# Token mixing: softmax division moved from GpSimd to ScalarE, three other wide element operations from GpSimd to VectorE

## The chip, the cores and the metric

One NeuronCore of a Trainium2 chip runs the kernel. Its engines work side by side, each through its own queue in order: TensorE (PE in the profile; its weight loads are PEld), VectorE (DVE), ScalarE (ACT), GpSimd (POOL) and SyncE (SP), which issues nearly all DMAs. The metric is device time in microseconds of one execution; the median of the runs counts.

## The reference

One layer of a streaming encoder, for a prompt of 2048 tokens and 8 sampled sequences of 16 tokens, model width 1024, all in float32:

```python
# x @ w_in gives q, k, v, output gate of 4 mLSTM heads (128 wide), 8 gate columns,
# and q (8 heads x 64), k, v (2 heads x 64) of a sliding-window attention
hm = mlstm_chunkwise(qm, km, vm, logi, logf, C0, n0, m0, chunk)   # matrix memory, exact per token
hm = sigmoid(om) * head_norm(hm)
qa, ka = rope(qa), rope(ka)
s = q k^T / 8, masked to the own chunk of 64 and two before
mx = max(max(s), sink);  p = exp(s - mx);  p = p / (sum(p) + exp(sink - mx));  ha = p v
h = layer_norm(alpha * x + concat(hm, ha) @ w_out)
u = h @ w_up;  c = causal conv of width 3;  f = (silu(c_gate) * c_value) @ w_down
y = layer_norm(alpha * h + f)
```

The outputs are y, the new memories and the last rows of keys, values and of u.

## The kernel before

A float32 product is made of three products of rounded numbers (a high and a low part of each side): the high part of a tile is a copy on ScalarE (L217, L562, L892), the low part a subtraction on VectorE (L218, L563, L893). The large products also save multiplications by a two by two scheme of sums of blocks, so their results are collected in three PSUM banks A, B and C that are evicted and added in a fixed order.

Tokens come in 17 tiles of 128 (16 of the prompt, one of the samples). Three stages follow each other on TensorE:

- the input projection (up to about 690 us) in four blocks of tiles. Its products are L700; `i_after` evicts the banks between them, on ScalarE (`i_out`'s L756 and L759, the copies L767, L775 and L795) and on VectorE (L771, L773). A product may begin only when the bank it writes has been evicted. Projected rows go to DRAM through SP (L749 for the attention queries, the output gate and v).
- the output projection and the first layer norm (about 690 to 960 us) in five blocks (L222 to L224, eviction L1607). `x_pair` (L880) loads pairs of mixed features and splits them.
- the feed-forward part, up-projection and down-projection (from 960 us).

The token mixing of each tile, mLSTM (`m_tile`, `m_norm`) and attention (`swa`), is woven between the matmuls of the first two stages: `Chains.weave` advances generators by an estimate of TensorE's time. This fixes the order of all TensorE instructions by hand; the order on the other engines is made by a planner that lays each instruction where its own estimate of times puts it. All small results of TensorE in the mixing share five PSUM banks in turn (`bank`), so a transposition may have to wait until a bank of an earlier step has been read.

Places that the change and the prediction touch:

- `swa`: `scores` makes masked scores and their maxima on VectorE (L1292 to L1297), `exps` the exponentials with their sums on ScalarE (L1301, L1303), `divided` adds the sink's part to the sums and takes the reciprocal on VectorE (L1306, L1307) and multiplies four heads by it on GpSimd (L1308). This is done twice a tile, for half of the heads each. TensorE then transposes the quotients (L1330) into banks called ppt.
- `m_tile`: VectorE makes sd and kw (L1122, L1191), GpSimd multiplies the queries by the weights of the state, qk by wi (L1192), TensorE uses both (L1199, L1200, L1207), VectorE reads the banks (statistics L1140, L1141, state L1210, values L1146). ScalarE's L1143 reads the same banks.
- `rope`: three products on VectorE (L864 to L866), and the sum on the engine that is handed in as `adder` (L867): VectorE for the keys of the prompt, GpSimd for the queries.
- `x_pair`: the low part (L893) on GpSimd for every second pair of the first four blocks, else on VectorE.

Of the kernel before, what the change touches and what calls it, by code (L numbers as in the profile page):

```python
# [8 lines left out]
F32 = mybir.dt.float32  # L9
F32R = mybir.dt.float32r  # L10
AF = mybir.ActivationFunctionType
# [3 lines left out]
P = 128  # L15
# [24 lines left out]
IBLOCKS = [[0, 1, 2, 3, 16], [4, 5, 6, 7], [8, 9, 10, 11], [12, 13, 14, 15]]  # L40
# [164 lines left out]
class Prog:  # L205
# [524 lines left out]
    def i_keys(self, b, ti, ps):  # L730
        nc = self.nc
        t = IBLOCKS[b][ti]
        kv = self.zev()[:, :2 * P]
        nc.scalar.copy(kv, ps[:, 8:264])
        nc.scalar.copy(self.gates[b][:, ti, :], ps[:, :8])
        self.rope(kv[:, :P], t, 1, nc.vector)
        nc.sync.dma_start(self.zkv[t], kv)

    def i_store(self, b, g, i, j, ev):
# [11 lines left out]
    def i_out(self, b, g, i, j, src):  # L751

        nc = self.nc
        ev = src if i else self.zev()
        if g == 3:
            nc.scalar.activation(ev, src, AF.Tanh, scale=0.5)  # L756
            nc.vector.tensor_scalar_add(ev, ev, 1.0)
        elif not i:
            nc.scalar.copy(ev, src)  # L759
        if g == 2:  # L760
            self.rope(ev, IBLOCKS[b][2 * j], 2, nc.gpsimd)
        self.i_store(b, g, i, j, ev)

    def i_after(self, b, g, s):
# [32 lines left out]
    def i_batch(self, g):  # L797

        nc = self.nc
        ps = self.sb.pop(g)  # L800
        t = NPT
        ev = self.zev()
        if g == 2:
            nc.scalar.copy(ev, ps)
            self.rope(ev, t, 1, nc.gpsimd)
            nc.sync.dma_start(self.zqa[t], ev)
            return
        if g < 2:
            nc.scalar.copy(ev[:, :HT], ps[:, :HT])
            nc.scalar.activation(ev[:, HT:], ps[:, HT:], AF.Copy, scale=KSCALE)  # L810
            self.trans = g, ev
            return
        if g == 3:
            nc.scalar.activation(ev, ps, AF.Tanh, scale=0.5)
            nc.vector.tensor_scalar_add(ev, ev, 1.0)
        else:
            nc.scalar.copy(ev, ps)
        nc.sync.dma_start((self.zog, self.zv)[g - 3][t], ev)
# [32 lines left out]
        nc.sync.dma_start(self.zt[0, k], x)  # L851
        nc.sync.dma_start(self.zt[1, k], y)

    def rope(self, A, t, nt, adder):

        V = self.nc.vector
        n = A.shape[-1]
        B = self.mp.tile([P, 512], F32, name="rb", tag="rb", bufs=1)[:, :n]
        r, i0 = self.angles[t]
        cos, ms, sin = [r[:, i0:i0 + nt, i:i + 1, :] for i in range(3)]  # L860
        w = A.rearrange("p (t x d) -> p t x d", t=nt, d=32)
        h = lambda z, s: z.rearrange("p (t h s d) -> p t h s d", t=nt, s=2, d=32)[:, :, :, s]
        over = lambda z: z.to_broadcast([P, nt, n // (64 * nt), 32])
        V.tensor_mul(h(B, 0), h(A, 1), over(ms))  # L864
        V.tensor_mul(h(B, 1), h(A, 0), over(sin))
        V.tensor_mul(w, w, cos.to_broadcast([P, nt, n // (32 * nt), 32]))  # L866
        adder.tensor_add(A, A, B)  # L867

    def rope_load(self, t, nt):

# [9 lines left out]
    def x_pair(self, b, p):  # L880

        nc, nb = self.nc, len(OBLOCKS)
        W = len(OBLOCKS[b]) * P
        if p == 0:
            for t in OBLOCKS[b]:
                self.chains.until(t)
        raw = self.xp.tile([P, 2, 512], F32, name="xraw", tag=f"xr{p + 1}", bufs=1)[:, :, :W]
        nc.sync.dma_start(raw, self.zmix[b][2 * p:2 * p + 2].rearrange("k p m -> p k m"))
        s = (7, 6, 5, 3, 4)[self.xn % 5]
        self.xn += 1  # L890
        h, l = [self.xp.tile([P, 2, 512], F32R, name=n, tag=f"{n}{s}", bufs=1)[:, :, :W] for n in ("oh", "ol")]
        nc.scalar.copy(h, raw)  # L892
        (nc.gpsimd if b < nb - 1 and p % 2 else nc.vector).tensor_sub(l, raw, h.bitcast(F32))  # L893
        self.xs.setdefault(b, []).extend((h[:, i], l[:, i]) for i in range(2))

    def group(self, b, tiles, u0, last):
# [278 lines left out]
    def m_tile(self, t, load, i, mp):  # L1175
        nc = self.nc
        V = nc.vector
        qk, v1, og = load
        pm = self.m_rep(i)
        col = self.m_cols(i, mp)  # L1180
        dt = self.m_masked(pm, self.mcau)
        yield 600, 2800
        emt = self.m_emt(col)
        wi = self.m_inter(pm, col)
        self.m_exps(dt, col)
        yield 0, 5000, 2
        ps = self.m_scores(qk)
        kt = self.m_ktok(qk)
        sd = self.m_weighted(ps, dt)
        kw = self.work("kw", [P, MH, P])  # L1190
        V.tensor_mul(kw, kt, dt[:, :, P - 1:P].to_broadcast([P, MH, P]))  # L1191
        nc.gpsimd.tensor_mul(qk[:, 0:4], qk[:, 0:4], wi)  # L1192
        yield 950, 4000, 4
        num = []
        for j in range(2):
            ps = self.bank([P, 2, 129], "pnum")
            for i in range(2):
                h = 2 * j + i
                nc.tensor.matmul(ps[:, i], sd[:, h], v1[:, h], start=True, stop=False)  # L1199
                nc.tensor.matmul(ps[:, i], qk[:, h], self.C[:, h], start=False, stop=True)  # L1200
            num.append(ps)
        Cn = self.work("C", [P, MH, 129], bufs=2)
        for j in range(2):
            ps = self.bank([P, 2, 129], "pcu")
            for i in range(2):
                h = 2 * j + i
                nc.tensor.matmul(ps[:, i], kw[:, h], v1[:, h], start=True, stop=True)  # L1207
            for i in range(2):
                h = 2 * j + i
                V.scalar_tensor_tensor(Cn[:, h], self.C[:, h], wi[:, h, P - 1:P], ps[:, i], op0=ALU.mult, op1=ALU.add)  # L1210
        self.C = Cn
        return num, emt, og
# [45 lines left out]
    def swa(self, t):  # L1258
        nc = self.nc
        V = nc.vector  # L1260
# [14 lines left out]
        N = nk * P  # L1275
        mix = self.work("mixa", [P, 4, P])

        def scores(j0):

            sink = [x.rearrange("p (k j) -> p k j", k=2)[:, :, j0:j0 + 2] for x in (self.sink, self.nsink)]  # L1280
            sc = self.work("sc", [P, 4, 2 * P], bufs=2)
            mx, es, sm = [self.work(n, [P, 4], bufs=2) for n in ("amx", "aes", "asm")]
            ps = [self.bank([P, 2, 2, P], "psc") for _ in range(2)]
            for j in range(2):
                for i, (q, k) in enumerate(((qh, self.kh), (qh, self.kl), (ql, self.kh))):
                    for kvh in range(2):
                        rs = slice(64 * kvh, 64 * kvh + 64)
                        nc.tensor.matmul(ps[kvh][:, j, :nk], q[rs, j0 + j], k[rs, sel], start=i == 0, stop=i == 2)  # L1288
            for kvh in range(2):
                for j in range(2):  # L1290
                    c = 2 * kvh + j
                    V.tensor_tensor_reduce(out=sc[:, c, :N], in0=ps[kvh][:, j, :nk].rearrange("p a b -> p (a b)"), in1=mask, scale=1.0, scalar=-3e38,  # L1292
                                           op0=ALU.add, op1=ALU.max, accum_out=mx[:, c:c + 1])

            w = lambda x: x.rearrange("p (k j) -> p k j", k=2)
            V.scalar_tensor_tensor(w(mx), w(mx), -0.125, sink[1], op0=ALU.mult, op1=ALU.min)
            V.tensor_add(w(es), sink[0], w(mx))  # L1297
            return sc, mx, es, sm

        def exps(sc, mx, es, sm):  # L1300
            nc.scalar.activation(es, es, AF.Exp)  # L1301
            for j in range(4):
                nc.scalar.activation(sc[:, j, :N], sc[:, j, :N], AF.Exp, bias=mx[:, j:j + 1], scale=0.125, accum_out=sm[:, j:j + 1])  # L1303

        def divided(sc, mx, es, sm):
            V.tensor_add(sm, sm, es)  # L1306
            V.reciprocal(sm, sm)  # L1307
            nc.gpsimd.tensor_mul(sc[:, :, :N], sc[:, :, :N], sm.rearrange("p (h o) -> p h o", o=1).to_broadcast([P, 4, N]))  # L1308

        z = [scores(0)]  # L1310
        yield 900, 3200, 2
        exps(*z[0])
        z.append(scores(2))
        yield 900, 3600
        divided(*z[0])
        exps(*z[1])
        if t + 1 < NPT and self.i_done > self.place(t + 1)[0]:
            self.a_load = self.swa_dma(t + 1)
        yield 0, 3000
        divided(*z[1])  # L1320
        scs = [x[0] for x in z]
        yield 0, 4200, 2 + 2 * (self.a_load is not None)
# [804 lines left out]
```

## Time and profile before

| | us |
|---|---|
| median of 3 runs | 2399.57 (2395.45 to 2402.28) |
| the profiled execution | 2395.7 |
| its span, first to last instruction | 2393.9 |

The profiled execution is 1.8 us longer than its span, and 3.9 us below the median. Of the span TensorE is busy 97%, VectorE 78%, ScalarE 52%, GpSimd 14%. A row of the groups reads: line, engine, operation, tile written and tiles read, shapes, count, then busy time in us and the mean duration in ns of one, then idle time of the engine just before, with who ended it. A row of waits reads: who waited, for whom, us in total, how often, the longest. A row of the stretches reads: the stretch, its length, then each engine's busy time with its count, the granted TensorE clock, the DMA share and GB/s. A row of the timeline reads: start, duration, engine, line, operation, and in brackets the idle time before it.

### The profile page before, as it was taken

How to read it: one execution, taken by the hardware profiler on the slowest of the kernel's cores; microseconds unless marked ns; L12 is line 12 of the kernel's file. 1: busy time of each engine (PE TensorE's matmuls, PEld its weight loads, DVE VectorE, ACT ScalarE, POOL GpSimd, SP SyncE). 2: the span in 40 equal slices, each digit the busy share in tenths (PEclk: the TensorE clock that was granted, in tenths of full speed). 3: DMA queues.
4: the chain of work that ended last, by engine and by line, in shares of the span. 5: the costliest groups of instructions: out<-in, count | busy, mean ns of one | idle time of the engine just before them, and what ended most of it. 6: DMA issues, size and time to landing. Idle time of an engine off the chain costs nothing.

```text
span 2393.9 us, 39845 instructions
## 1 busy us (share of the span) xinstructions
PE 2326.6 (97%) x14425; PEld 2128.9 (89%) x14425; DVE 1860.4 (78%) x3180; ACT 1233.6 (52%) x2295; POOL 347.1 (14%) x354
## 2 busy tenths in 40 slices
PE   8999999999999999999999999999999999999998
PEld 8999998988887777999999999999999978778776
DVE  8676587687789897987788777768766786895987
ACT  5453455655554444655556555455544544544553
POOL 0101103112222331300000000002100100310400
PEclk9999999999999999999999999999999999999999
DMA  8798888789877656687776889888988786756652
GB/s 287 261 315 291 280 294 311 261 263 328 288 247 241 204 197 240 252 308 281 283 271 240 312 315 316 306 270 269 318 284 262 227 284 203 233 174 223 226 172 106
DMA packets 296934, 624.98 MB, mean 261 GB/s; under 512 B 47005, under 2 KB 140193, under 8 KB 296737
## 3 DMA queue, kind: packets, MB, share of 16 engines
q1 hardware_dynamic: 294144, 612.99, 75.3%
q0 software_dynamic: 1728, 6.29, 0.7%
q10 hardware_dynamic: 864, 3.15, 0.3%
q8 instruction: 114, 1.87, 0.3%
q14 instruction: 84, 0.68, 0.1%
HBM read 451.78 MB, written 170.56 MB: 260 GB/s over the span
## 4 chain that ended last, share of the span: by engine, by line
PE 68%; DVE 10%; DMA 4%; issue 3%; ACT 2%; POOL 1%; SPq 0%; DVEq 0%; POOLq 0%; ACTq 0%
PE dps L1830 18%; PE fup L1830 17%; PE dps L700 6%; PE fht L2033 5%; PE dps L2033 5%; PE fup L2033 4%; PE dps L222 2%; PE dps L223 2%; PE dps L224 2%; DMA txy<-wdn 1%; DVE w L218 1%; DVE uw L218 1%; PE ppo L1336 1%; PE ppt L1330 1%; PE psc L1288 1%
## 5 line engine op out<-in xcount | busy, mean ns | idle before, releaser
L1830 PE MATMUL dps<-hh,uw 128*128 128x384 f32 (+1 forms) x1848 | 481.6, 329 | 7.0 <-ACT u L1855 1.9
L1830 PE MATMUL fup<-hh,uw 128*128 128x384 f32 (+1 forms) x1848 | 479.9, 328 | 2.0 <-ACT u L1855 1.8
L1830 PEld LDWEIGHTS dps<-hh,uw 128*128 128x128 f32 x1848 | 330.1, 188 | 10.8 <-ACT u L1855 3.0
L1878 DVE SCALAR_TENSOR_TENSOR cc<-u,cw,cc 128x768 f32<-128x768 f32 (+1 forms) x264 | 252.5, 977 | 106.6 <-ACT cc L1876 104.7
L1830 PEld LDWEIGHTS fup<-hh,uw 128*128 128x128 f32 x1848 | 330.1, 188 | 2.8 <-ACT u L1855 2.4
L1830 PE MATMUL fup<-hl,uw 128*128 128x384 f32 (+1 forms) x924 | 302.9, 328 | 1.5 <-DVE hl L218 1.5
L1830 PE MATMUL dps<-hl,uw 128*128 128x384 f32 (+1 forms) x924 | 302.5, 327 | 0.0
L700 PE MATMUL dps<-w,oh 128*128 128x256 f32 x1344 | 258.2, 286 | 9.4 <-DMA w<-zws 3.2
L218 DVE TENSOR_TENSOR w<-wraw,w 128x1024 fp32r<-128x1024 f32 (+2 forms) x167 | 207.0, 1247 | 55.7 <-ACT w L217 53.1
L217 ACT CAST w<-wraw 128x1024 fp32r<-128x1024 f32 (+2 forms) x167 | 162.8, 986 | 140.1 <-PE dps L700 54.2
L700 PEld LDWEIGHTS dps<-w,oh 128*128 128x128 f32 x1344 | 212.5, 189 | 22.2 <-issue 8.9
L217 ACT CAST uw<-wraw 128x1024 fp32r<-128x1024 f32 x126 | 122.9, 978 | 197.1 <-PE dps L2033 99.3
L218 DVE TENSOR_TENSOR uw<-wraw,uw 128x1024 fp32r<-128x1024 f32 x126 | 150.7, 1197 | 62.9 <-ACT uw L217 62.6
L1876 ACT ACTIVATE cc<-u,cw 128x768 f32<-128x768 f32 (+1 forms) x132 | 129.6, 997 | 121.6 <-DVE u L1869 61.4
L700 PE MATMUL dps<-w,ol 128*128 128x256 f32 x672 | 188.7, 281 | 0.0
L2033 PE MATMUL fup<-uw,fu 128*128 128x512 f32 x726 | 177.7, 400 | 9.5 <-ACT fht L2040 6.9
L2033 PEld LDWEIGHTS fup<-uw,fu 128*128 128x128 f32 x726 | 137.8, 191 | 44.7 <-ACT fht L2040 7.8
L700 PE MATMUL dps<-oh,w 128*128 128x256 f32 x896 | 169.1, 284 | 7.4 <-ACT dps L775 3.1
L1830 PEld LDWEIGHTS fup<-hl,uw 128*128 128x128 f32 x924 | 173.5, 188 | 2.3 <-DVE hl L218 2.3
L1830 PEld LDWEIGHTS dps<-hl,uw 128*128 128x128 f32 x924 | 173.5, 188 | 0.0
L2033 PE MATMUL dps<-uw,fu 128*128 128x512 f32 x660 | 165.0, 395 | 0.0
L700 PEld LDWEIGHTS dps<-oh,w 128*128 128x128 f32 x896 | 141.4, 190 | 13.5 <-issue 4.1
(328 smaller groups left out, 4699.9 us busy)
## 6 DMA issues: line engine op xcount, KB each, us to landing
uw<-zw SPq DMA_DIRECT2D x176, 512.0 KB, 4.6
zw<-uw SPq DMA_DIRECT2D x88, 512.0 KB, 2.9
w<-zws SPq DMA_DIRECT2D x72, 512.0 KB, 6.3
wv<-wup SPq DMA_DIRECT2D x66, 512.0 KB, 5.5
wraw<-wi SPq DMA_DIRECT2D x65, 512.0 KB, 5.6
wraw<-zt SPq DMA_DIRECT2D x60, 512.0 KB, 4.3
wraw<-wdn SPq DMA_DIRECT2D x45, 512.0 KB, 4.0
wraw<-wo SPq DMA_DIRECT2D x40, 512.0 KB, 4.7
```

The costliest lines, as they stand in the source:

```text
L217: nc.scalar.copy(hi, src)
L218: nc.vector.tensor_sub(lo, src, hi.bitcast(F32))
L222: mm(out, ah, bh, start=start, stop=False)
L223: mm(out, ah, bl, start=False, stop=False)
L224: mm(out, al, bh, start=False, stop=stop)
L700: mm(o, l, r, start=s in (1, 7) and c == k == i == 0, stop=k == 3 and i == 2, skip_group_check=True)
L1288: nc.tensor.matmul(ps[kvh][:, j, :nk], q[rs, j0 + j], k[rs, sel], start=i == 0, stop=i == 2)
L1330: nc.tensor.transpose(pp[:, j * P:(j + 1) * P], scs[j // 2][:, 2 * kvh + j % 2, kt * P:(kt + 1) * P], self.ident)
L1830: mm(ps, l[:, k], r[:, k], start=s in (1, 7) and k == 0 and i == 0, stop=k == 3 and i == 2, skip_group_check=True)
L1876: S.activation(c[:, v], u[:, v, 2:2 + n], AF.Identity, bias=w[3], scale=w[2])
L1878: V.scalar_tensor_tensor(c[:, v], u[:, v, i:i + n], w[i], c[:, v], op0=ALU.mult, op1=ALU.add)
L2033: mm(ps, l[:, k, c], r[:, k], start=s in (1, 4, 7) and u == 0 and k == 0 and i == 0, stop=u == nu - 1 and k == n - 1 and i == 2, skip_grou ...
```

## The change

```diff
 def i_keys / i_out / i_batch
-        self.rope(kv[:, :P], t, 1, nc.vector)
+        self.rope(kv[:, :P], t, 1)
-            self.rope(ev, IBLOCKS[b][2 * j], 2, nc.gpsimd)
+            self.rope(ev, IBLOCKS[b][2 * j], 2)
-            self.rope(ev, t, 1, nc.gpsimd)
+            self.rope(ev, t, 1)
 def rope
-        adder.tensor_add(A, A, B)
+        V.tensor_add(A, A, B)
 def x_pair
-        (nc.gpsimd if b < nb - 1 and p % 2 else nc.vector).tensor_sub(l, raw, h.bitcast(F32))
+        nc.vector.tensor_sub(l, raw, h.bitcast(F32))
 def m_tile
-        nc.gpsimd.tensor_mul(qk[:, 0:4], qk[:, 0:4], wi)
+        V.tensor_mul(qk[:, 0:4], qk[:, 0:4], wi)
 def swa
         def divided(sc, mx, es, sm):
             V.tensor_add(sm, sm, es)
             V.reciprocal(sm, sm)
-            nc.gpsimd.tensor_mul(sc[:, :, :N], sc[:, :, :N], sm.rearrange("p (h o) -> p h o", o=1).to_broadcast([P, 4, N]))
+            for j in range(4):
+                nc.scalar.activation(sc[:, j, :N], sc[:, j, :N], AF.Copy, scale=sm[:, j:j + 1])
...
         yield 900, 3600
-        divided(*z[0])
         exps(*z[1])
+        divided(*z[0])
```

The rotation's sum, every low part of `x_pair` and the multiplication of the queries run on VectorE. The division of the softmax becomes four scaled copies on ScalarE, one for each head, and the first half's division is issued after the exponentials of the second half. The planner then lays the instructions of VectorE, ScalarE, GpSimd and SP of the first two stages anew; the order on TensorE is the same in all its 8461 rows, and from the feed-forward part on the order is the same on all engines. GpSimd keeps the narrow operations (powers for the norms, small copies, memsets), and three lines of the sample tile (L1388, L1427, L1497). Lines behind L1308 stand one further down in the changed kernel, where the four copies are L1309.

More of the change, by code (lines that the diff above doesn't have):

```diff
@@ L852, in d_sums, with rope @@
         nc.sync.dma_start(self.zt[1, k], y)
-    def rope(self, A, t, nt, adder):
+    def rope(self, A, t, nt):
         V = self.nc.vector
@@ L1314, in swa @@
         yield 900, 3600
+        exps(*z[1])
         divided(*z[0])
-        exps(*z[1])
         if t + 1 < NPT and self.i_done > self.place(t + 1)[0]:
```

## Prediction

> **What bounds the kernel now.** I read the page's first part, the stretches, and then TensorE's waits.
>
> ```profile
> PE 2326.6 (97%) x14425; PEld 2128.9 (89%) x14425; DVE 1860.4 (78%) x3180; ACT 1233.6 (52%) x2295; POOL 347.1 (14%) x354
> ```
> ```profile
> 230.00:690.00 460.00, 444.23 (x3607) 409.87 (x3606) 338.83 (x930) 257.32 (x652) 91.17 (x68) 0.99 0.88 292
> 690.00:960.00 270.00, 257.87 (x1395) 200.68 (x1394) 232.99 (x529) 133.80 (x333) 82.38 (x49) 0.97 0.62 212
> 400.00:425.00 25.00, 20.93 (x167) 20.47 (x166) 21.06 (x62) 10.37 (x26) 12.24 (x9) 0.93 0.82 289
> 775.00:800.00 25.00, 21.47 (x121) 17.96 (x120) 24.97 (x51) 11.84 (x26) 13.96 (x7) 0.93 0.53 179
> 850.00:875.00 25.00, 19.61 (x102) 16.45 (x101) 25.00 (x50) 11.85 (x26) 13.13 (x6) 0.86 0.55 192
> 875.00:900.00 25.00, 25.00 (x132) 18.84 (x132) 21.36 (x59) 10.84 (x38) 8.78 (x6) 0.94 0.54 192
> ```
>
> TensorE is busy 97% of the span, so only its gaps can be won. Between 230 and 960 us, where nearly all of the change lies, it is idle 730 - 444.2 - 257.9 = 28 us. The worst stretches are those where GpSimd is busy 12 to 14 of 25 us, and in two of them VectorE is busy all the time. There the granted clock falls as well: 25 x (1 - 0.93) = 1.75 us lost at 775, 3.5 at 850 and 1.5 at 875, 6.75 together, and 1.75 at 400. Who ends the gaps:
>
> ```profile
> PE ppt L1330 <- DVE C L1210: 8.8, 3, 4.5
> PE dps L700 <- ACT zev L767: 3.7, 4, 1.4
> PE dps L700 <- ACT zev L759: 3.3, 2, 2.7
> ```
>
> The largest item, three gaps at 719, 792 and 865 us, is TensorE waiting for a PSUM bank that VectorE has yet to read. The timeline shows why VectorE is late there, first its own rows, then GpSimd's:
>
> ```profile
> 858.38 3.22 DVE L218 TENSOR_TENSOR w<-wraw,w 128x1024 fp32r<-128x1024 f32 x1
> 861.52 2.91 DVE L1557 SCALAR_TENSOR_TENSOR ymix<-ymix,lsc,o_ln_b 128x1024 f32<-128x1024 f32 x1
> 864.36 3.38 DVE L893 TENSOR_TENSOR ol<-xraw,oh 128x1024 fp32r<-128x1024 f32 x1
> 867.66 1.21 DVE L218 TENSOR_TENSOR w<-wraw,w 128x1024 fp32r<-128x1024 f32 x1
> 868.79 1.12 DVE L1210 SCALAR_TENSOR_TENSOR C<-C,wi,pcu 128x129 f32<-128x129 f32 x4
> ```
> ```profile
> 858.16 2.36 POOL L893 TENSOR_TENSOR ol<-xraw,oh 128x1024 fp32r<-128x1024 f32 x1
> 860.48 2.88 POOL L1308 TENSOR_TENSOR sc<-sc,asm 128x1024 f32<-128x1024 f32 x1
> 863.32 3.33 POOL L893 TENSOR_TENSOR ol<-xraw,oh 128x1024 fp32r<-128x1024 f32 x1
> ```
>
> The two engines take turns. L218 takes 3.22 us while GpSimd works and 1.21 us 9 us later, and ends 1.1 us after GpSimd's instruction (860.52); so does L1557 (863.36, 864.43). VectorE's "busy" time holds waiting for GpSimd.
>
> The Trainium skill (SBUF — State Buffer, section Who interferes with whom) says it so: a VectorE instruction with two SBUF inputs and a GpSimd instruction that reads SBUF share one read interface, and the second to come is held for the whole of the first. By that rule, the trace agrees: 3.22 against 1.21 us.
>
> **The change part by part.** What leaves GpSimd, the four rows that the change takes away:
>
> ```profile
> L1308 POOL TENSOR_TENSOR sc<-sc,asm 128x1024 f32<-128x1024 f32 (+1 forms) x32 | 64.2, 2009 | 237.0 <-DVE asm L1307 80.4 <-DMA zt<-txy 45.6 <-DVE aes L1297 27.9
> L867 POOL TENSOR_TENSOR zev<-zev,rb 128x512 f32<-128x512 f32 x17 | 27.3, 1607 | 139.8 <-DMA qk<-zqk 94.1 <-DVE zev L866 34.3 <-ACT zev L767 6.9
> L1192 POOL TENSOR_TENSOR qk<-qk,wi 128x512 f32<-128x512 f32 x16 | 23.8, 1487 | 28.2 <-ACT sc L1303 14.4 <-issue 8.5 <-DVE asm L1307 4.7
> L893 POOL TENSOR_TENSOR ol<-xraw,oh 128x1024 fp32r<-128x1024 f32 (+1 forms) x8 | 22.6, 2824 | 8.9 <-ACT oh L892 8.9
> ```
>
> That is 64.2 + 27.3 + 23.8 + 22.6 = 138 us of GpSimd. What VectorE gets for it, and what it is freed of, by its groups from 230 to 960 us and, for four lines of the whole span, their shortest, median and longest duration:
>
> ```profile
> L218 DVE TENSOR_TENSOR w<-wraw,w 128x1024 fp32r<-128x1024 f32 x93 | 131.1, 1414 | 27.1 <-ACT w L217 24.8 <-DMA zqk<-zev 1.2 <-DMA zmix<-mixa 0.7
> L893 DVE TENSOR_TENSOR ol<-xraw,oh 128x1024 fp32r<-128x1024 f32 x6 | 13.8, 2300 | 2.1 <-ACT oh L892 2.1
> L1296 DVE SCALAR_TENSOR_TENSOR amx<-amx,nsink 128x4 f32<-128x4 f32 x32 | 13.3, 417 | 0.4
> L1297 DVE TENSOR_TENSOR aes<-k_sink,amx 128x4 f32<-128x4 f32 x32 | 12.2, 381 | 0.5
> L1191 DVE TENSOR_TENSOR kw<-pkt,dt 128x512 f32<-128x512 f32 x16 | 10.8, 676 | 0.0
> ```
> ```profile
> L218 DVE TENSOR_TENSOR w<-wraw,w x167: 418/1217/3393, 5.5 to 952.8; 128x1024 fp32r<-128x1024 f32 x143, 128x528 fp32r<-128x528 f32 x20, 128x256 fp32r<-128x256 f32 x4
> L1296 DVE SCALAR_TENSOR_TENSOR amx<-amx,nsink x32: 134/162/2364, 321.9 to 894.3; 128x4 f32<-128x4 f32 x32
> L1297 DVE TENSOR_TENSOR aes<-k_sink,amx x32: 144/162/1250, 323.2 to 895.2; 128x4 f32<-128x4 f32 x32
> L1557 DVE SCALAR_TENSOR_TENSOR ymix<-ymix,lsc,o_ln_b x15: 1262/1276/2910, 708.7 to 947.6; 128x1024 f32<-128x1024 f32 x15
> ```
>
> - Added: 17 sums (L867) and 16 products (L1192) of 512 columns at L1191's 0.676 us, 22.3 us; eight low parts (L893), six of 1024 columns at L218's median of 1.22 and two of 768 at three quarters of it, 9.2 us. Together 31.5 us.
> - Freed: mean less median, times count. L218 (1.414 - 1.217) x 93 = 18.3; L1296 (0.417 - 0.162) x 32 = 8.2; L1297 the same way 7.0; L893 (2.300 - 1.22) x 6 = 6.5. These four give 40 us; a little of it is the sample tile's, which stays.
>
> So VectorE becomes some 8 us lighter although it does more. What it loses to GpSimd is densest where both are busy, around 715, 790 and 860 us; the rotation's sums fall into the input projection, where VectorE has a quarter of its time free (338.8 of 460 us busy). None of the three added kinds waits for an engine that VectorE did not wait for before: the rotation's sum follows its own product, the queries' weights wi are made on ScalarE ahead of the dt that L1122 and L1191 already need, and the low part waits for its high part as the even pairs' do. The last is the one new place where VectorE can stand for ScalarE (L892), with all its queue behind it; the row of L893 above shows 2.1 us of such waiting for the pairs that are there already, so four pairs more may cost about 2 us, within the bounds below.
>
> - **The three bank gaps.** At 865 us the chain ahead of L1210 shrinks by (3.22 - 1.22) + (2.91 - 1.28) + (3.38 - 1.22) = 5.8 us, and the added products cost 0.68 + 1.22 = 1.9 us: 3.9 us of a gap of 4.5. Late next are the quotients: in some tiles the new order puts the second reciprocal behind L1146, and ScalarE's second four copies behind L1143, which waits for VectorE. I take 6.2 of the 8.8 us. Of the clock's 6.75 us, which stand beside gaps over 3 us, I take 5.4. Sum 11.6 us; bounds 0 and 15.6.
> - **The rotation's sums.** SP issues a store of rotated queries when GpSimd is done, and loads of weights stand behind it.
>
> ```profile
> SPq L749 <- POOL zev L867: 41.7, 15, 6.5
> ```
> ```profile
> 407.88 0.39 SPq L480 DMA_DIRECT2D w<-zws  x1
> 411.47 0.80 SPq L749 DMA_DIRECT2D zqa<-zev  x2
> 412.36 1.36 SPq L480 DMA_DIRECT2D w<-zws  x3
> 410.15 1.29 POOL L867 TENSOR_TENSOR zev<-zev,rb 128x512 f32<-128x512 f32 x1
> 417.66 0.80 PE L700 MATMUL dps<-w,oh 128*128 128x256 f32 x2 [2.63 <-DMA w<-zws]
> ```
>
> SP stood 3.2 us, and TensorE then waited 2.63 us for that weight and lost 1.75 us of clock. On VectorE the sum follows L866 directly, 0.68 us later. I take 3 of these 4.4 us. No DMA is added or removed.
>
> - **The division on ScalarE.** 128 copies, 120 of 256 columns.
>
> ```profile
> L1303 ACT ACTIVATE sc<-sc,amx 128x256 f32<-128x256 f32 x120 | 59.7, 499 | 38.1 <-DVE amx L1296 32.2 <-DVE asm L1307 4.6 <-DVE asm L1306 1.3
> L1159 ACT ACTIVATE hn<-hn,ms 128x128 f32<-128x128 f32 x68 | 21.9, 390 | 40.0 <-DVE ms L1157 39.8
> ```
>
> The same kind of copy with 128 columns costs 21.9 / 68 = 0.32 us, an exponential of 256 costs 0.50; I take 0.42, nearer the exponential in width, 1.7 us for four, 53 us in all (bounds 41 and 64). ScalarE has room: busy 391 of 730 us. But it is in order, and in the input projection the new order puts copies directly ahead of evictions (L756, L759, L767) in eight places. Those already cost TensorE 3.7 + 3.3 us. An eviction has the time of a product of 24 matmuls, and 30 took 3.53 us:
>
> ```profile
> 606.44 3.53 PE dps L700 x30
> ```
>
> that is 2.8 us less some 0.6 of its own, so 2.2 us of slack. Four copies fit where the eviction is not late already. I take +4 us; bounds 0 and 8 x 1.7 = 13.6.
>
> **Sum.** -11.6 - 3 + 4 = -10.6 us. The profiled execution took 2395.7, its span plus 1.8, and lies 3.9 under the median of 2399.6; the differences apply to the median: 2399.6 - 10.6 = 2389.
>
> **The rivals.**
>
> 1. ScalarE's queue becomes the bound; slower. GpSimd waited 80.4 us for the reciprocal (L1307, in the row of L1308), and nothing stood behind it. ScalarE has evictions behind it. The point from which it decides: 2.2 us of lateness. If in the eight places the copies come 1.7 us late and wait another 2.2 us for VectorE, each costs 1.7, and five of them cost 1.75 us of clock: 13.6 + 8.8 = 22 us against 11.6 won: 2410. For it: the evictions in TensorE's waits. Against it: VectorE, and with it the reciprocal, runs earlier. Chance 0.21.
> 2. VectorE stays full and the gain does not arrive: the 31.5 us added fall into the stretches that are full (24.97 and 25.00 of 25), the time freed elsewhere; gaps move and keep their sum. 2400, chance 0.21. This is how it would be if L218's 3.22 us had another cause than GpSimd.
> 3. All of it arrives: 15.6 + 4.4 us without a loss on ScalarE gives 2380, and a few gaps of the input projection more, 2376. Chance 0.13.
>
> The Trainium skill (Perfetto Trace Analysis, section Optimizing Scalar/DVE Operations) speaks against this change in one sentence: where VectorE is saturated, moving work to ScalarE or even GpSimd may help; here work goes to VectorE. That is rival 2. The same section warns that moving between VectorE and GpSimd may not help because they share a port.
>
> **Numbers.** My forecast holds 2380 to 2392, chance 0.45. Under 0.3% (7.2 us) a measurement of this kernel tells nothing from no change. Faster 0.45 + 0.13 = 0.58, same 0.21, slower 0.21. The range goes from rival 3 to rival 1, 2375 to 2409.
>
> **What would show it.** Right: L218's longest near 1.23 us before 960 us; L1296's mean near 0.16; the wait of ppt for L1210 under 3 us; clock 1.00 from 850 to 875; SP's waits at L749 shorter; VectorE busy some 10 us less from 230 to 960 and ScalarE 53 more. Wrong: TensorE's waits for L756 to L767 above 10 us, ScalarE waiting for L1307 ahead of its copies, ppt waiting for the copies, or VectorE's durations unchanged.

## The result, and the profile after

The changed kernel takes 2364.49 us (2361.58 to 2366.53) against 2399.81 us (2395.45 to 2402.28) for the kernel before: ratio 0.985, 95% interval 0.983 to 0.987. It is 35 us faster, where 11 were forecast; the time lies below the whole predicted range. The two profiled executions differ by less, 29.1 us of span, since that of before was one of its quicker ones and that of after one of its slower ones.

First the page's line of engines, then the same stretches of work. Of the two stretches, the first row holds the input projection and the second the output projection: they hold 3606 and 1396 matmuls, one less and one more than 230 to 690 and 690 to 960 us held before. The last rows stand in the two places where VectorE was full before, and the down-projection.

```profile
PE 2316.2 (98%) x14425; PEld 2122.7 (90%) x14425; DVE 1834.5 (78%) x3221; ACT 1284.3 (54%) x2423; POOL 209.4 (9%) x281
```
```profile
230.00:676.00 446.00, 439.66 (x3606) 407.86 (x3605) 329.60 (x953) 288.34 (x732) 16.70 (x24) 0.99 0.90 302
676.00:930.00 254.00, 252.13 (x1396) 197.13 (x1395) 214.28 (x541) 152.72 (x381) 29.39 (x25) 1.00 0.67 225
775.00:800.00 25.00, 25.00 (x142) 18.97 (x140) 22.08 (x63) 15.49 (x51) 3.94 (x3) 1.00 0.58 207
850.00:875.00 25.00, 25.00 (x145) 20.01 (x144) 23.69 (x72) 13.90 (x44) 3.52 (x2) 1.00 0.45 158
...
2060.00:2085.00 25.00, 21.53 (x87) 16.92 (x86) 24.44 (x24) 11.17 (x15) 10.84 (x7) 0.93 0.74 244
```

The input projection became 14 us shorter (460 to 446), the output projection 16 us (270 to 254). TensorE's idle time in the two fell from 27.9 to 6.3 + 1.9 = 8.2 us. Another 8.5 us is clock: the trace's clock record has five pieces of 3.41 us and one of 10.24 us at half speed in these stages before (13.6 us lost) and three of 3.41 us after (5.1 lost). Together that is 28 of the 30 us by which the two stretches became shorter. What follows takes as long as before within 1 us.

The shortest, median and longest duration of the lines that the prediction named, and TensorE's waits that are left:

```profile
L218 DVE TENSOR_TENSOR w<-wraw,w x167: 415/1217/1571, 5.7 to 922.9; 128x1024 fp32r<-128x1024 f32 x143, 128x528 fp32r<-128x528 f32 x20, 128x256 fp32r<-128x256 f32 x4
L1296 DVE SCALAR_TENSOR_TENSOR amx<-amx,nsink x32: 131/155/166, 322.7 to 863.7; 128x4 f32<-128x4 f32 x32
L1297 DVE TENSOR_TENSOR aes<-k_sink,amx x32: 132/154/164, 323.4 to 864.3; 128x4 f32<-128x4 f32 x32
L1309 ACT ACTIVATE sc<-sc,asm x128: 385/496/512, 326.4 to 870.7; 128x256 f32<-128x256 f32 x120, 128x128 f32<-128x128 f32 x8
```
```profile
PE fup L2034 <- ACT fht L2041: 6.9, 2, 3.5
PE dps L700 <- ACT zev L759: 3.7, 1, 3.7
PE dps L700 <- ACT dps L775: 2.8, 1, 2.8
```

L1296, a row of four columns that once took 2.36 us, never takes more than 0.17. L218's longest falls from 3.39 to 1.57 us; the 1.57 lies under a GpSimd product of the sample tile (L1498), which stayed. The wait for L1210 is gone from the list, and none for the copies took its place. The largest wait left, for L2041, is in the down-projection, with the clock at 0.93; there, in the row of 2060 us, GpSimd is busy 10.8 of 25 us.

### The profile page after: what moved, and what is told of

Same layout as the page of the kernel before. It is cut to its first block, busy times and chain, and to the rows that moved or that the text cites. A ratio compares the mean times of both kernels' runs of the same rounds, so it can differ in the third digit from the quotient of the medians.

```text
span 2364.8 us, 39830 instructions
## 1 busy us (share of the span) xinstructions
PE 2316.2 (98%) x14425; PEld 2122.7 (90%) x14425; DVE 1834.5 (78%) x3221; ACT 1284.3 (54%) x2423; POOL 209.4 (9%) x281
## 4 chain that ended last, share of the span: by engine, by line
PE 69%; DVE 7%; DMA 3%; issue 2%; ACT 1%; POOL 1%; SPq 0%; DVEq 0%; POOLq 0%; ACTq 0%
PE dps L1831 18%; PE fup L1831 18%; PE fht L2034 5%; PE dps L700 5%; PE dps L2034 5%; PE fup L2034 3%; PE dps L222 2%; PE dps L224 2%; PE dps L223 2%; PE ppo L1337 1%; DVE uw L218 1%; PE ppt L1331 1%; PE psc L1288 1%; DVE hl L218 1%; DMA yacc<-zh 1%
## 5 line engine op out<-in xcount | busy, mean ns | idle before, releaser
L218 DVE TENSOR_TENSOR w<-wraw,w 128x1024 fp32r<-128x1024 f32 (+2 forms) x167 | 189.1, 1139 | 56.2 <-ACT w L217 53.6
L700 PEld LDWEIGHTS dps<-w,oh 128*128 128x128 f32 x1344 | 213.4, 190 | 14.6 <-issue 8.9
L218 DVE TENSOR_TENSOR uw<-wraw,uw 128x1024 fp32r<-128x1024 f32 x126 | 150.7, 1198 | 63.4 <-ACT uw L217 63.1
```

Source lines behind the costliest of these rows:

```text
L218: nc.vector.tensor_sub(lo, src, hi.bitcast(F32))
L700: mm(o, l, r, start=s in (1, 7) and c == k == i == 0, stop=k == 3 and i == 2, skip_group_check=True)
```

## Experiments

Two theories of the gain were put against each other. The first: wide GpSimd instructions hold VectorE, and through it TensorE. The second: nothing is held that matters, and the gain comes from elsewhere, be it results that no longer queue on GpSimd, or the planner's new order, or quotients that come in smaller pieces. Where "the port" stands below, it is short for the first: VectorE held by what GpSimd reads. "Stretched time" below is, over all VectorE instructions that overlap a given GpSimd line, the duration less the 20th percentile of the same line and shape; an instruction that overlaps several lines counts under the one that it overlaps longest. Before, it was 27.0 us under L1308, 12.5 under L893, 11.3 under L1192 and 4.2 under L867, 55 us. After, these lines are no longer GpSimd's, and some 5 us are left in the first two stages, nearly all under the sample tile's products.

Each ratio is to the kernel before as it ran beside that row's kernel, where its median lay between 2397.3 and 2399.8 us; so differences between rows by medians and by ratios differ by up to some 4 us.

| run | us | ratio to before | 95% interval |
|---|---|---|---|
| the change | 2364.5 | 0.9854 | 0.9835 to 0.9873 |
| p_div: division only | 2369.2 | 0.9891 | 0.9876 to 0.9906 |
| p_rope: rotation's sums only | 2395.0 | 0.9992 | 0.9982 to 1.0002 |
| p_qk: queries' product only | 2398.0 | 1.0006 | 0.9995 to 1.0017 |
| p_low: low parts only | 2384.1 | 0.9952 | 0.9939 to 0.9966 |
| p_three: all but the division | 2382.3 | 0.9932 | 0.9919 to 0.9945 |
| lock_read: change, idle reads of 512 | 2374.4 | 0.9905 | 0.9886 to 0.9923 |
| lock_write: change, idle writes of 512 | 2362.5 | 0.9856 | 0.9835 to 0.9876 |
| joint: control of the next | 2366.1 | 0.9860 | 0.9837 to 0.9883 |
| lock_wide: idle reads of 1024 | 2378.1 | 0.9912 | 0.9889 to 0.9935 |
| pdiv_read: p_div, idle reads | 2381.1 | 0.9925 | 0.9913 to 0.9938 |
| pdiv_write: p_div, idle writes | 2370.7 | 0.9889 | 0.9874 to 0.9904 |
| act_double: change, copies twice | 2366.7 | 0.9868 | 0.9855 to 0.9882 |
| div_v: division on VectorE, wide | 2379.9 | 0.9930 | 0.9915 to 0.9946 |
| div_v4: the same, by head | 2376.4 | 0.9911 | 0.9897 to 0.9925 |
| p_three4: division on GpSimd by head | 2385.9 | 0.9956 | 0.9944 to 0.9969 |
| ffn_v: change, and L1569 on VectorE | 2351.4 | 0.9807 | 0.9788 to 0.9826 |
| best2: ffn_v, and the sample tile | 2352.9 | 0.9818 | 0.9804 to 0.9831 |

### The port by itself

GpSimd gets work that nobody needs and nobody waits for, and all other engines keep their order. If VectorE is held, the time must rise; if the work matters for its result alone, it can't.

```diff
 # lock_read, against the changed kernel (in divided)
             V.reciprocal(sm, sm)
+            for x in (qh, ql):
+                nc.gpsimd.tensor_sub(x, x.bitcast(F32), sm.rearrange("p (h o) -> p h o", o=1).to_broadcast([P, 4, P]))
 # lock_write instead
+            nc.gpsimd.tensor_copy(mx, sm)
+            for x in (qh, ql):
+                nc.gpsimd.memset(x.bitcast(F32), 0.0)
```

> The changed kernel, and behind each second reciprocal of the softmax two GpSimd instructions of 128x512 that read the split queries, which nobody needs any more, and write them back: 64 instructions for which nobody waits. The order on TensorE, VectorE, ScalarE and SP is that of the changed kernel, row by row. If VectorE is held by wide GpSimd instructions that read SBUF, and this held the kernel up, then L218's longest is again near 3 us before 960 us, VectorE's busy time rises by some 25 us, and the time rises towards the kernel before: 27 of the 55 us by which VectorE's instructions were stretched in the mixing lay under the division, so 17 of the 35 us come back, 2381 us (2372 to 2390). If the gain came because results no longer queue on GpSimd, or because the planner laid the other engines anew: nothing, 2364.5 within 5 us.

> The same, with one narrow copy of 4 columns and two memsets of 128x512 on GpSimd in place of the two that read: GpSimd is as busy, and the order of the other engines is again that of the changed kernel. If reading SBUF is what holds VectorE: 2364.5 within 4 us, L218 at 1.22 us. If a busy GpSimd slows the others whatever it does: as in the run with reads, 2372 us or more.

The engines' busy time and L218's durations, lock_read first, lock_write second:

```profile
PE 2320.5 (98%) x14425; PEld 2125.0 (90%) x14425; DVE 1857.5 (78%) x3221; ACT 1286.6 (54%) x2423; POOL 293.3 (12%) x345
```
```profile
L218 DVE TENSOR_TENSOR w<-wraw,w x167: 419/1221/2061, 5.5 to 925.8; 128x1024 fp32r<-128x1024 f32 x143, 128x528 fp32r<-128x528 f32 x20, 128x256 fp32r<-128x256 f32 x4
```
```profile
PE 2314.1 (98%) x14425; PEld 2121.0 (90%) x14425; DVE 1835.1 (78%) x3221; ACT 1286.8 (55%) x2423; POOL 257.9 (11%) x377
```
```profile
L218 DVE TENSOR_TENSOR w<-wraw,w x167: 418/1222/1576, 5.4 to 916.6; 128x1024 fp32r<-128x1024 f32 x143, 128x528 fp32r<-128x528 f32 x20, 128x256 fp32r<-128x256 f32 x4
```

VectorE runs the same 3221 instructions in the same order in both. With the reads its busy time is 23 us more than in the changed kernel (23.7 us of stretched time under the added line), and the kernel is 10 us slower (12 by the ratios). L218's longest is 2.06 us, not near 3. With the writes nothing happens to either, though GpSimd is busy 48 us more (in 29 of the 32 halves the memsets began before the reciprocal; the narrow copies ran behind it). So reading is what holds VectorE, and it costs the kernel time. By the Trainium skill (SBUF — State Buffer, section Who interferes with whom), a GpSimd instruction that only writes does not contend with a VectorE instruction of two SBUF inputs; the trace agrees, 0.5 us of stretched time under the copies and memsets.

The expected 17 us did not come back in full, so the same was tried in the shape of the division itself, one instruction of 1024 columns. For that the high and low parts of the queries lie in one tile; joint has only this.

```diff
 # joint
-        qh, ql = self.work("qh", [P, 4, P], F32R), self.work("ql", [P, 4, P], F32R)
+        qb = self.work("qb", [P, 8, P], F32R); qh, ql = qb[:, :4], qb[:, 4:]; self.qb = qb
...
 # lock_wide, besides
             V.reciprocal(sm, sm)
+            qb = self.qb.rearrange("p (h a) o -> p h (a o)", a=2)
+            nc.gpsimd.tensor_sub(qb[:, :, :N], qb[:, :, :N].bitcast(F32), sm.rearrange("p (h o) -> p h o", o=1).to_broadcast([P, 4, N]))
```

> A control for the next run: the changed kernel with the split queries' high and low parts laid beside each other in one tile of 1024 columns, and nothing else. The order on the engines is the changed kernel's but for some 30 places around the sample tile: 2364.5 within 4 us.

> That control with one GpSimd instruction of 1024 columns behind each second reciprocal, in place of the two of 512 tried before: the division's own shape, reading and writing split queries that nobody needs, with nobody waiting. If VectorE held by GpSimd is the whole of the 18 us between the kernel with three parts (2382.3) and the changed one: 2380 or more, VectorE's stretched time near the 31 us it had there. If it gives back 10 us like the two narrower ones: 2374, and 8 us are the new order's or the quotients' own way.

lock_wide is 12 us slower than joint, with 29.6 us of stretched time. One place of it in its timeline:

```profile
841.79 1.90 POOL L1307 TENSOR_TENSOR qb<-qb,asm 128x1024 fp32r<-128x1024 f32 x1 [11.48 <-DVE asm L1306]
841.82 2.94 DVE L1556 SCALAR_TENSOR_TENSOR ymix<-ymix,lmv,o_ln_g 128x1024 f32<-128x1024 f32 x1
```

The layer norm's row takes 2.94 us when it starts 0.03 us behind a GpSimd read that no one needs. In the changed kernel the same row takes 1.27 (831.96, further below). The two intervals are wide against the differences, so "10 to 12 us" is what idle reads at the division's places cost the changed kernel, and not a figure to the microsecond.

### The parts alone

```diff
 # p_div: of the change only the hunk in swa    # p_rope: only rope's sum
 # p_qk: only m_tile's product                  # p_low: only x_pair's low part
 # p_three: p_rope, p_qk and p_low together
```

> The kernel before, with the division alone on ScalarE (and the exponentials of the second half ahead of it). By the port: VectorE was stretched by 27 of 55 us under L1308, half of the 35 us, 2382 us. By the prediction's own terms for this part: four copies 4 us late, against some part of the bank gaps won, 2395 to 2403. If ScalarE's queue delays evictions: above 2403.

> The kernel before, with the rotation's sums (L867) alone on VectorE. By the prediction: SP no longer stands for GpSimd, 3 of 4.4 us, 2396. By the port alone: 4.2 us of stretched instructions leave, 11.5 are added, 0 to -3 us. If the stores' wait on SP was what held the input projection in more places than the one at 414 us: 2390 or less.

> The kernel before, with the queries' product (L1192) alone on VectorE: 10.8 us added, 11.3 us of stretched instructions gone. By the port: 0 to -7 us (11.3 / 55 x 35), 2392 to 2399. If VectorE's full stretches only get fuller: 2399 or more.

> The kernel before, with all low parts of x_pair (L893) on VectorE: 9.2 us added, 12.5 us of stretched instructions gone, nearly all of them in the output projection. By the port: -8 us (12.5 / 55 x 35), the gap at 865 us smaller, 2391. If the added subtractions stand for ScalarE's high parts (L892) at the head of VectorE's queue: 2399 or more.

> The kernel before with the other three parts on VectorE and the division left on GpSimd. The single parts sum to -13.2 - 2.3 + 0.7 = -14.8 us, 2382.5. By the stretched time, 28 of 55 us gone: -17, 2380. If the division was the part without which the others give little: 2388 to 2396.

The division alone brings 28 us, the low parts 13, the other two nothing that can be told from zero. The three small parts sum to -15, and p_three has -16; with the division it would be -43, and the change has -35. So the division's move is worth 28 us by itself and 18 on top of the others. p_div came out 13 us below the 2382 that its expectation worked out from stretched time. Its two stages:

```profile
230.00:675.00 445.00, 439.36 (x3600) 405.49 (x3599) 321.98 (x922) 285.43 (x729) 51.76 (x48) 0.99 0.89 300
675.00:929.00 254.00, 251.42 (x1392) 196.41 (x1391) 218.33 (x534) 153.16 (x385) 56.44 (x37) 1.00 0.66 227
```

The order on TensorE is the same in all these kernels. Counted between the same matmuls, p_div's input projection is 14 us shorter and its output projection 15, nearly as much as the whole change gains in each (14 and 16). p_low's output projection is 10 us shorter, its input projection not at all. The two parts win some of the same time in the output projection, which is why they don't add up.

p_rope shows why the rotation's sums were the wrong item. Rows of its timeline at the place of the stall at 414 us:

```profile
409.19 2.22 POOL L1308 TENSOR_TENSOR sc<-sc,asm 128x1024 f32<-128x1024 f32 x1 [5.62 <-DVE asm L1307]
409.69 2.27 DVE L867 TENSOR_TENSOR zev<-zev,rb 128x512 f32<-128x512 f32 x1
...
411.99 0.89 SPq L749 DMA_DIRECT2D zqa<-zev  x2
...
412.97 1.35 SPq L480 DMA_DIRECT2D w<-zws  x3
...
418.48 0.50 PE L700 MATMUL dps<-w,oh 128*128 128x256 f32 x2 [2.12 <-DMA w<-zws]
```

The sum, whose product of the same shape takes 0.68 us (L1191), takes 2.27 us under the division; SP's store goes out at 411.99 (411.47 before), and TensorE still waits 2.12 us for the weight (2.63 before). In the kernel before, the sum had stood behind the same division on GpSimd's queue. Once the division is gone (p_div), TensorE's longest wait between 367 and 779 us is 1.1 us, although GpSimd still makes the sums.

### GpSimd's queue, ScalarE's load, and the quotients' way

```diff
 # pdiv_read, pdiv_write: the idle reads and writes of lock_read and lock_write, in p_div
 # act_double, against the changed kernel
-                nc.scalar.activation(sc[:, j, :N], sc[:, j, :N], AF.Copy, scale=sm[:, j:j + 1])
+                [nc.scalar.activation(sc[:, j, :N], sc[:, j, :N], AF.Copy, scale=z) for z in (sm[:, j:j + 1], 1.0)]
 # div_v, against the changed kernel
+            V.tensor_mul(sc[:, :, :N], sc[:, :, :N], sm.rearrange("p (h o) -> p h o", o=1).to_broadcast([P, 4, N]))
 # div_v4 instead
+            for j in range(4):
+                V.tensor_scalar_mul(sc[:, j, :N], sc[:, j, :N], sm[:, j:j + 1])
 # p_three4, against p_three
+            [nc.gpsimd.tensor_mul(sc[:, j, :N], sc[:, j, :N], sm[:, j:j + 1].to_broadcast([P, N])) for j in range(4)]
```

> The kernel with the division alone on ScalarE (2369.2 us), and behind each second reciprocal the same two GpSimd instructions of 128x512 that read and write split queries nobody needs. All other engines keep that kernel's order. It brings back what GpSimd did to the others by the division (holding VectorE, and keeping the other three kinds of work behind it on GpSimd's queue), but not the order and not the results' way. If that is the whole of the 28 us that the division alone gained: 2390 to 2400. If the port costs here what it cost in the changed kernel, 10 us: 2379. If the gain lay in the new order or in the quotients' way: under 2375.

> The same with the narrow copy and two memsets of 128x512, which wait on GpSimd for the same reciprocal and keep the same work behind them, but read nothing wide. If GpSimd's queue is the part beyond the port (sums of the rotation, queries and low parts behind a division that waits): 2378 or more. If only reading counts: 2369 within 4 us.

Idle reads in p_div cost 12 us by the medians (8 by the ratios). Idle writes cost 1.5, within the interval, although GpSimd's narrow copy waits 60 us in all for the reciprocal (the division waited 80). Work queued behind a waiting instruction on GpSimd is not what cost.

The reads give back only 8 to 12 of the 28 us that the division's move gains alone, though with them VectorE's stretched time between 230 and 960 us is 45 us, against 24 in p_div and 54 before. The other 16 to 20 us stay open: p_div also has the planner's new order, the second half's exponentials ahead of the first division, and quotients that ScalarE makes head by head, and no run takes these apart.

> The changed kernel with each of the 128 copies done twice (the second with a factor of 1): 57 us more on ScalarE, as much again as the change put there. It prices the load that the prediction charged with 4 us. If ScalarE has room where the copies stand: 2364.5 within 5 us. If evictions and exponentials stand behind the copies: 2372 or more, and had the first lot cost the same, the change without this price would have been as much faster still.

Another copy of every quotient costs 2 us by the medians (3 by the ratios), and the intervals overlap. The load was less than expected:

```profile
PE 2316.3 (98%) x14425; PEld 2121.8 (90%) x14425; DVE 1834.3 (78%) x3221; ACT 1320.4 (56%) x2551; POOL 212.0 (9%) x281
```

ScalarE is busy 36 us more than in the changed kernel, not 57; the change itself had put 51 there. The quotients also come later: from the reciprocal's end to the end of the last copy of the first two heads it is 2.10 us in the changed kernel and 3.26 in act_double, means over the 32 halves. Neither 36 us more on ScalarE nor 1.2 us of lateness meets a limit here. The planner laid the other engines anew in this run, so the 2 us are not the copies' alone.

> The changed kernel, with the division on VectorE as one product of 1024 columns a half tile instead of four copies on ScalarE: 32 more instructions of some 1.27 us on VectorE, 40 us, and 53 to 62 us less on ScalarE; GpSimd as in the changed kernel. If freeing the shared port was all that mattered: 2364.5 within 6 us, since VectorE has 130 us idle in its 730. If VectorE is the bound of the stretches at 720, 790 and 860 us, their gaps come back by some 1.3 us for each product in them with the clock's loss: 2372 to 2385 us. If ScalarE's copies delay the evictions ahead of the transpositions: faster, 2358.

> The changed kernel with the division on VectorE as four products of 256 columns by one number each, in place of one of 1024 (2379.9 us). If VectorE's load is what costs there: 2379 within 5 us, as the columns are the same. If heads that come one by one are what ScalarE's form brought: 2370 or less.

> The three parts on VectorE and the division on GpSimd, but as four products of 256 columns, one for each head, in place of one of 1024. TensorE's transpositions can begin with two heads. If the 18 us that still lie between that kernel (2382.3) and the changed one are quotients that come in one late piece, TensorE's waits for them, 8 us, shrink: 2372 or less. If it is VectorE held by GpSimd's reads, the same columns are read: 2382 within 5 us, more if four instructions cost GpSimd more than one.

On VectorE the division costs 15 us against ScalarE (12 by head). VectorE is not held there either (0.8 us of stretched time between 230 and 960 us), but it carries 32 us more (1866.1 against 1834.5 us busy), and in div_v TensorE waits for the quotients:

```profile
PE ppt L1331 <- DVE sc L1309: 4.8, 2, 2.4
```

That VectorE's load is the whole of the 15 us is not shown, since the planner's order differs here too. By head on GpSimd it is no faster: the four pieces halve VectorE's stretched time (14.6 us against 31.1) but take GpSimd 4 x 0.85 = 3.4 us instead of 2.1, and TensorE's waits for the quotients do not shrink (9.5 us after 8.0):

```profile
PE ppt L1330 <- POOL sc L1308: 8.0, 4, 2.9
```
```profile
PE ppt L1330 <- POOL sc L1308: 9.5, 11, 1.7
```

(p_three first, p_three4 second.) These waits tell where the 4 to 8 us may lie by which p_three is slower than the changed kernel with idle reads. In p_three VectorE and GpSimd hold each other on the way to one transposition:

```profile
840.25 1.90 POOL L1308 TENSOR_TENSOR sc<-sc,asm 128x1024 f32<-128x1024 f32 x1 [11.01 <-DVE asm L1306]
840.28 2.94 DVE L1555 SCALAR_TENSOR_TENSOR ymix<-ymix,lmv,o_ln_g 128x1024 f32<-128x1024 f32 x1
...
849.81 0.13 DVE L1307 RECIPROCAL asm<-asm 128x4 f32<-128x4 f32 x1
849.94 1.19 DVE L893 TENSOR_TENSOR ol<-xraw,oh 128x1024 fp32r<-128x1024 f32 x1
850.11 2.76 POOL L1308 TENSOR_TENSOR sc<-sc,asm 128x1024 f32<-128x1024 f32 x1 [6.48 <-DVE bmv L1141]
...
850.50 0.38 PE L1330 MATMUL ppt<-ident,sc 128*128 128x128 f32 x2
...
852.93 0.33 PE L1330 MATMUL ppt<-ident,sc 128*128 128x128 f32 x1 [2.05 <-POOL sc L1308]
```

The same place of the changed kernel:

```profile
831.96 1.27 DVE L1556 SCALAR_TENSOR_TENSOR ymix<-ymix,lmv,o_ln_g 128x1024 f32<-128x1024 f32 x1
...
839.80 0.14 DVE L1307 RECIPROCAL asm<-asm 128x4 f32<-128x4 f32 x1
839.94 1.21 DVE L893 TENSOR_TENSOR ol<-xraw,oh 128x1024 fp32r<-128x1024 f32 x1
...
840.85 1.71 ACT L1309 ACTIVATE sc<-sc,asm 128x256 f32<-128x256 f32 x4
...
841.74 1.20 PE L1331 MATMUL ppt<-ident,sc 128*128 128x128 f32 x8
```

In p_three L1555 is held 1.67 us, and VectorE works without a break from there to the second reciprocal; then the product itself is held by L893 (2.76 us where the first one took 1.90), and TensorE's third transposition, the first that needs the second half, waits 2.05 us. In the changed kernel all eight run through without a gap. An idle read makes VectorE late, and the quotients less so (in lock_wide this wait is 0.99 us). Such pairs may account for the rest, but no run separates it from the planner's order, which differs between p_three and the change; it stays open.

### A faster version

If the port is what costs, the down-projection should gain as well: there the last sum of the second layer norm (L1569 of the changed kernel), 12 instructions of 1024 columns, is on GpSimd in both kernels. The list of what GpSimd keeps, under "The change", leaves these out.

```diff
 # ffn_v, against the changed kernel
-            yield from self.norm_steps(ys[t], *ln2, V if end else nc.gpsimd)
+            yield from self.norm_steps(ys[t], *ln2, V)
 # best2, besides: the sample tile's L1389, L1428 and L1498 on nc.vector
```

> The changed kernel, and in the down-projection the last sum of the second layer norm (L1569, 12 instructions of 128x1024 on GpSimd, 36 us) on VectorE too. In the changed kernel VectorE's instructions are stretched by 21.7 us under these 12; as VectorE's own they cost 12 x 1.22 = 14.6 us. If the port theory holds there as well, the two stalls at 2068 and 2235 us (3.6 us each, with 3.4 us at half clock each) go, 7 + 3.4 us: 2354 us (2352 to 2360). If these stalls have another cause (ScalarE's order, or GpSimd's late results): 2364.5 within 4 us.

> The changed kernel with the last sum of the second layer norm on VectorE (2351.4 us), and the sample tile's three wide products (L1389, L1428, L1498) there too: 4.6 us of stretched instructions of VectorE gone, some 9 us added. By the port: 2348 to 2352. If they stand ahead of work that TensorE waits for near 155 to 180 us: 2355 or more.

ffn_v takes 2351.4 us: 13 us less than the changed kernel, 46 less than the one before, the fastest of all that ran, and 0.6 us below the range that was expected. Its stretches of the two old stalls:

```profile
2050.00:2075.00 25.00, 24.56 (x105) 19.44 (x104) 24.04 (x33) 15.23 (x19) 5.12 (x6) 1.00 0.79 281
2220.00:2245.00 25.00, 25.00 (x109) 19.97 (x108) 24.37 (x32) 12.30 (x17) 3.08 (x4) 1.00 0.70 251
```

VectorE is as full as in the changed kernel's stretch at 2060 (24 of 25 us) but does 33 and 32 instructions in it instead of 24. The wait of TensorE for ScalarE's L2041 fell from 6.9 to 0.4 us in the down-projection: the culprit was neither of the two engines that the wait names. Nor were GpSimd's sums late for anybody on TensorE's path. In the changed kernel only the store of y waits for L1569:

```profile
  POOL y L2071: 3.6, 12
```

best2 removes nearly the last of the stretched time (1.0 us left in the whole kernel) and gains nothing more: 2352.9, intervals overlapping. The sample tile's products stood where nothing waited.

## Why the prediction was wrong

The direction was right, and VectorE held by GpSimd's reads is a cost that the runs confirm. The size was off by a factor of three, -35 against -10.6 us. The step that failed is the sum's term for the division: it stands there as a cost of 4 us, and the division's move gains 28 us alone and 18 on top of the other parts. A second term, the rotation's sums, had the wrong cause.

- **The three bank gaps**, -11.6 us within 0 to 15.6. The gaps went entirely, and the clock at 850 us is 1.00: the waits for L1210 are gone and the output projection is 16 us shorter, the upper bound and not the value taken. (The clock's loss was said to stand beside gaps over 3 us; the two are 2.9 and 4.5.) "Late next are the quotients" held for p_three, where 8.0 us of waits for L1308 appear, but not for the changed kernel: the copies on ScalarE come early enough there, and with each done twice TensorE waits 1.3 us for them.
- **The rotation's sums**, -3 us. The cause was wrong: SP stood for GpSimd, but GpSimd's sum stood behind the division (L1308, 407.97 to 410.19 us; the sum starts at 410.15), and on VectorE it stands under it. Alone this part gives 2.3 us, not told apart from none. The input projection's 14 us came with the division's move, also where GpSimd kept the sums (p_div). For the same reason the prediction's words that nothing stood behind the division on GpSimd are wrong; pdiv_write shows that this queue cost nothing that can be told.
- **The division on ScalarE**, +4 us within 0 to 13.6. This is the largest mistake. The prediction booked the division as a cost on ScalarE and gave the gain to the gaps that name VectorE; alone, the division's move gains 28 us. Of these, 8 to 12 are VectorE held by GpSimd's reads, as the idle reads show; the cause of the rest stays open. The price of ScalarE's time was near the lower bound: 36 us more of load cost 2 us. 53 us more of ScalarE was right (50.7): a copy's median is 0.50 us, but the copies overlap, and four in a row take 1.71 us as forecast.
- **VectorE's ledger**, 40 us freed for 31.5 added. It counted four lines; these have 40.1 us of stretched time, but all lines together have 55 (L1557 2.8, L865 2.0, L1306 1.9, L1555 1.7 and smaller ones), and VectorE's busy time fell by 25.9 us, not by 8. The "four pairs more" of low parts that wait for L892 are eight, by the prediction's own count of what is added. Their waits grew from 2.1 to 4.7 us, about the 2 us that it forecast.
- **Why the input projection was missed.** There VectorE was a quarter idle, and TensorE's waits named ScalarE and DMAs; so VectorE's delay was priced only where it was full. But ScalarE waits in order for VectorE, with evictions behind it. Two rows of before:

```profile
402.00 1.24 DVE L1296 SCALAR_TENSOR_TENSOR amx<-amx,nsink 128x4 f32<-128x4 f32 x1
...
403.28 0.51 ACT L1303 ACTIVATE sc<-sc,amx 128x256 f32<-128x256 f32 x1 [2.74 <-DVE amx L1296]
```

and the same two of the changed kernel:

```profile
401.29 0.15 DVE L1296 SCALAR_TENSOR_TENSOR amx<-amx,nsink 128x4 f32<-128x4 f32 x1
...
401.81 0.50 ACT L1303 ACTIVATE sc<-sc,amx 128x256 f32<-128x256 f32 x1
```

The maxima took 1.24 us beside GpSimd's L1192 (401.76 to 403.22 us), and the row ahead of them, L865, took 0.74 instead of 0.42 under the end of L1308. So the exponentials started at 403.28 instead of 401.81; the eviction L767 comes behind them, and TensorE stood 1.45 us for it (until 405.97). This is one gap; the others of the input projection were not followed one by one.

- **Rival 1** (ScalarE's queue becomes the bound) did not happen, and in act_double 36 us more did not bring it about. **Rival 2** (VectorE stays full) did not happen either: from 775 and from 850 us VectorE is busy 22.1 and 23.7 of 25 us, where it was full before (the work there is not quite the same, as the changed kernel is ahead by then). div_v gives an idea of how it would have been with 32 us more on VectorE. **Rival 3** had the right sign of what was missing and still stopped 12 us short, because its bounds came from the named gaps alone. (The range's ends, 2375 and 2409, lie 1 us off the rivals' 2376 and 2410.)

Of the signs named beforehand, L1296's mean, the wait for L1210, the clock at 850 us, shorter waits of SP for the sums (41.7 us before, 16.7 after) and ScalarE's 53 us came as written; L218's longest is 1.57 because of the sample tile. VectorE's busy time in the two stages fell by 28 us, not by 10. One sign of being wrong came too: ScalarE waits for L1307 ahead of its copies, 9.9 us in nine waits, but no wait of TensorE for the copies follows.

## What to carry to other kernels

Compare the duration of one kind of instruction with its own minimum: here a narrow row that took ten times its median was held by a neighbour, and the engine's busy share said nothing of it. Price such a delay through every engine that waits in order behind the held one, not only in the gaps that name it. Of the places tried for this division, ScalarE with four scaled copies was the fastest (2364 us), ahead of VectorE (2376 and 2380) and GpSimd (2382 and 2386). And before a cost is booked for the engine that takes the work, put the work on it twice and see, and read from the trace how much load that really added.

## What the runs showed of the hardware

- A VectorE instruction of four columns (L1296) was held up to 2.36 us, until the end of GpSimd's instruction:

```profile
778.27 3.17 POOL L893 TENSOR_TENSOR ol<-xraw,oh 128x1024 fp32r<-128x1024 f32 x1 [1.33 <-ACT oh L892]
779.10 2.36 DVE L1296 SCALAR_TENSOR_TENSOR amx<-amx,nsink 128x4 f32<-128x4 f32 x1
```

  All six of its rows of over 0.3 us in the kernel before end 0.02 us behind an instruction of GpSimd. Behind a wide read that started 0.03 us earlier, a row of 1024 columns took 2.94 us in place of 1.27.
- It goes both ways: GpSimd's product of 1024 columns took 2.76 us when a VectorE subtraction had started 0.17 us earlier, 1.90 when it started first. GpSimd's memsets and narrow copies, 48 us of them, left VectorE's times as they were (0.5 us of stretched time).
- TensorE's gaps of 3.5 us in the down-projection cost more than themselves: each of the two is followed by 3.41 us at half clock in the trace's record, 1.7 us more. With the gaps gone (ffn_v) the clock stays at 1.00 there.
